# A transformer block on one core: attention and output projection in an order computed by a list scheduler at build time, and one merged score product for the first query tile

## The chip, the cores and the metric

The kernel runs on one core of a Trainium2 chip. A core has several engines that work side by side and wait for each other through semaphores: TensorE (PE in the profile, with its weight loads as PEld), VectorE (DVE), ScalarE (ACT), GpSimd (POOL) and SyncE (SP), which here issues the DMA transfers. The metric is the time of one execution on the device in microseconds; lower is better.

## The reference

One block of a transformer with 512 tokens (T) of width 1024, batch 1. Half of its 16 heads are "NSA" heads with three branches (compressed keys, selected keys, window), half attend within a sliding window of 128 with a learned sink. After attention come the output projection, a gated MLP with a short convolution, and a gated side input p.

```python
h = rmsnorm(x, attn_pre_g)
q_n, kc, vc, ksl, vsl, kwn, vwn, g_n, q_s, k_s, v_s = split(h @ w_in)
k_cmp, v_cmp = compress_kv(kc, ...), compress_kv(vc, ...)   # 31 blocks of 32 tokens
gates = sigmoid(g_n)
# NSA, per query: scores = q.k / 8 - slope * distance, causal
o_nsa = gates[0] * softmax(q k_cmp) v_cmp + gates[1] * softmax(q k_slc) v_slc \
      + gates[2] * softmax(q k_win) v_win
# sliding window: softmax over 128 keys and a sink in the denominator
o_swa = softmax([q_s k_s, sink]) v_s
x = x + rmsnorm(concat(o_nsa, o_swa) @ w_o, attn_post_g)
h = rmsnorm(x, mlp_pre_g)
a, u = split(h @ w_gate_up)
y = (gelu(causal_conv3(a)) * u) @ w_down
x = x + rmsnorm(y, mlp_post_g)
x = x + (p @ w_ple) * sigmoid(x @ w_ple_gate)
```

With 512 tokens there are 8 blocks to select from and 16 may be selected, so the selected branch sees every causal key, as the window of 512 does. 8 NSA heads share 2 key and value heads, and so do the 8 sliding-window heads. All is in float32.

## The kernel before, in words

**Numbers.** A float32 product is made of three products of rounded parts (`fp32r`): high with high, low with high, high with low (`mm3`, L147, L150, L151). So each weight is loaded raw (L140, tag `wr`, two buffers), its high part is cast on ScalarE (L128), and the low part is a difference on VectorE or GpSimd (L132). TensorE multiplies 128 rows by up to 512 columns into one PSUM bank.

**Stages.** Input and the natural-order values (to 33 us of the span), compression, key projections and the first three query projections (to 72), attention with the rest of the projections and the first half of the output projection (72 to 225), the second half of the output projection (225 to 249.5), the normalisation with the e = p·w_ple tiles (to 262), then the MLP and the gate.

**Attention.** 16 units are worked through: for NSA, and then for the sliding window, key group g = 0 and 1, and for each the query tiles qt = 3, 0, 2, 1 (128 queries, 4 heads each).

- *Scores* (`nsa_scores`, `swa_scores`). Two TensorE products per score piece, q with the high and the low part of the keys (L568, L569; `score`), into one of three PSUM banks (tag `s`). An NSA head's keys stand side by side in one tile `kn`: 32 compressed, 512 selected, 512 window keys. VectorE adds the distance bias and takes the minimum in one pass (L627, L595 for the window heads), ScalarE takes the exponential (L631), VectorE the reciprocal of the sum, GpSimd scales each row by it and by the gate (L537).
- *Values* (`pv`). Per 128 keys TensorE transposes the four heads' probabilities into one of two PSUM banks (L515, four transposes), ScalarE copies the high part out (L517), VectorE makes the low part (L519), and TensorE multiplies both with the values into the unit's one output bank (L548, two products per key block). `put_out` folds the output bank: a ScalarE copy (L526), two VectorE adds (L531), a ScalarE cast (L533) and a GpSimd difference (L534).

**What sets the order.** Each unit's scores and an earlier unit's value products are Python generators. `together` interleaves them by hand-written keys. After each step it calls `fill(ns)`, which adds credit at a hand-set rate (`RATES`, one for each group of units) and, while credit lasts, issues steps of 650 ns of the `fillers`: the projections of features 3, 8, 4, 5, 6, 7 (8 is the window keys; their results' low part on GpSimd in L389, then moved into place by DMAs on SP, L244), and after the first window unit `out_proj_first`. `pin` ties the first matmul of a filler step behind the attention step that was issued six steps earlier (`LAG`). Within those ties and the data's dependencies the framework's own scheduler, which simulates the engines, decides the order on each engine at build time. `keep_in_program_order` holds an instruction to the written order; in this part it is hardly used.

**Output projection.** For each of 8 columns c, `out_proj_first` sums k = 0 to 3 (the NSA half) and ScalarE copies the bank to `mo` (L798); `out_proj` then sums k = 4 to 7 and VectorE adds it (L827). Products are at L782 to L784. Each half column of the weight (`wo`, 256 KB) goes through `wr`, cast and difference (GpSimd in the first half, VectorE in the second). ScalarE squares the column (L236) and GpSimd sums the squares (L237; the last on VectorE) for the norm. In the second half, `ple_load` (p transposed and the two 512 KB weights `wple`, through `wr`) is called after c = 2, the reload of x (L241, four transfers of 512 KB) after c = 4.

Of the kernel before, what the change touches and what calls it, by code (L numbers as in the profile page):

```python
# [59 lines left out]
FILL_STEP = 650.0  # L60
WARM = 9
RATES = [0.36, 0.36, 0.9, 0.6]
LAG = 6
CYC = ["s", "o", "t", "t", "s", "mm", "s", "mm"]


class Block:
    def __init__(self, tc, io, ctx):
# [17 lines left out]
        self.fillers = []  # L86
        self.credit = 0.0
        self.rate = 1.0
        self.steps = [None]
        self.pinned = None  # L90
# [52 lines left out]
    def mm3(self, ps, wt, off, x, start, stop, keep=False):  # L143
# [3 lines left out]
        r = self.pin(mm(ps, hi, x[:, 0, :], start=start, stop=False))  # L147
# [4 lines left out]

    def pin(self, r):

        if self.pinned is not None:
            self.tc.add_manual_dep(r.ins, self.pinned.name, mybir.DependencyInfo(
                mybir.DependencyClass.NoSync, mybir.DependencyReason.DATA), reason="filler")
        return r
# [10 lines left out]


    def fill(self, ns):

        self.credit += ns * self.rate
        self.steps.append(self.steps[-1])
        while self.credit > 0 and self.fillers:
            self.credit -= FILL_STEP
            self.fill_step()

    def fill_step(self):
        phase, self.phase = self.phase, "fill"  # L180
        self.pinned = self.steps[max(0, len(self.steps) - 1 - LAG)]
        try:
            next(self.fillers[0])
        except StopIteration:
            self.fillers.pop(0)
        self.pinned = None
        self.phase = phase

    def drain(self, gen):
        while any(f is gen for f in self.fillers):  # L190
            self.fill_step()

    def att(self, r):
        self.steps[-1] = r.ins
        return r
# [180 lines left out]
    def proj(self, wt, f=None):  # L376
# [11 lines left out]
        eng = nc.gpsimd if self.phase == "fill" else nc.vector  # L388
        eng.tensor_sub(t[:, 1, :], v, t[:, 0, :].bitcast(F32))  # L389
# [91 lines left out]
    def compress_out(self, hk, hv):  # L481
# [13 lines left out]
        for g in range(2):  # L495
            z = [self.kn[g][i][:, 31:32] for i in range(2)]
            for a in z:
                nc.vector.memset(a.bitcast(F32), 0.0)
            hi, lo = self.kn[g][0][:, 0:31], self.kn[g][1][:, 0:31]
# [10 lines left out]
    def transpose_split(self, srcs, rows=P):  # L510

        nc = self.nc
        pt = self.ps("t")
        for r, src in enumerate(srcs):
            self.att(nc.tensor.transpose(pt[:rows, r * P : (r + 1) * P], src, self.ident))  # L515
# [23 lines left out]
    def pv(self, blocks, mix, qt):  # L539
# [22 lines left out]
        if last:  # L562
            product(n - 1, 1, False, True)
# [832 lines left out]
```

## Time and profile before

| | us |
|---|---|
| median of 3 runs (664.89 to 665.47) | 665.14 |
| the profiled execution's own time | 668.27 |
| its span | 666.5 |
| TensorE busy in the span | 652.6 (98%) |
| VectorE / ScalarE / GpSimd busy | 480.7 / 363.1 / 147.4 |
| attention, first score to the end of its half of the output projection | 72.3 to 225.2 |
| second half of the output projection | 225.2 to 249.5 |
| normalisation and e tiles | 249.5 to 262.0 |

A chain of waits is read from the top: a piece's start, its length, the engine or DMA that carried it, and its line. In a group, the numbers behind the first bar are the sum in us and the mean in ns, those behind the second the idle time ahead of the instructions and what ended it. In the timeline the bracket holds the idle time ahead of one instruction. All times of the profile are those of one execution; engines' "busy" counts a matmul from its issue on, with a modelled end.

### The profile page before, as it was taken

To read this page: it belongs to the slowest core of one execution; us is meant where nothing else is said; L and a number is where in the kernel's file an instruction comes from. 1 tells how busy PE (TensorE), PEld (TensorE's weight loads), DVE (VectorE), ACT (ScalarE), POOL (GpSimd) and SP (SyncE) were. 2 spreads that over 40 slices of the span, in tenths; PEclk is the share of its full clock that TensorE was granted. 3 is DMA by queue.
4 is the path that set the end of the run, shared out by engine and by line. 5 is a ranking of instruction groups with operands and counts; after the bars stand their busy time and mean duration, and the time that the engine had idled before them with its cause. 6 is when DMAs were issued, how large, how long until landed. Compare 5 with 4: busy or idle time off the path is not lost.

```text
span 666.5 us, 10339 instructions
## 1 busy us (share of the span) xinstructions
PE 652.6 (98%) x3741; PEld 565.5 (85%) x3741; DVE 480.7 (72%) x965; ACT 363.1 (54%) x684; POOL 147.4 (22%) x223
## 2 busy tenths in 40 slices
PE   8999999999999999999999999999999999999996
PEld 7988768777888777888887999999998888889985
DVE  6795777878757757858999999999958333224872
ACT  6554688878868737445555565565736323222351
POOL 1021568558556241003221000000000000001000
PEclk9999999999999999999999999999999999999999
DMA  8346721111121557412241332332244554332031
GB/s 299 115 139 213 199 64 47 34 48 49 48 73 56 179 206 269 173 57 95 95 160 63 127 109 83 128 117 76 95 144 156 153 209 143 88 111 71 1 127 63
DMA packets 27282, 78.01 MB, mean 117 GB/s; under 512 B 3424, under 2 KB 4704, under 8 KB 27232
## 3 DMA queue, kind: packets, MB, share of 16 engines
q1 hardware_dynamic: 27088, 77.28, 35.6%
q8 instruction: 29, 0.48, 0.3%
q14 instruction: 21, 0.17, 0.1%
q10 hardware_dynamic: 144, 0.08, 0.0%
HBM read 63.72 MB, written 6.29 MB: 105 GB/s over the span
## 4 chain that ended last, share of the span: by engine, by line
PE 79%; DVE 11%; ACT 4%; DMA 2%; issue 2%; POOL 1%; ACTq 0%; DVEq 0%
PE nsa_pso L548 3%; PE mlpdown_pss L147 3%; PE mlpdown_pss L150 3%; PE mlpdown_pss L151 3%; PE strassen_pss L1080 3%; PE strassen_pss L1084 2%; PE strassen_pss L1083 2%; PE nsa_pst L515 2%; PE mlpdown_psmm L147 2%; PE mlpdown_psmm L150 2%; PE mlpdown_psmm L151 2%; DMA outproj_wr<-in_wo_dram 2%; PE strassen_pst L1080 2%; PE strassen_pst L1083 2%; PE strassen_pst L1084 2%
## 5 line engine op out<-in xcount | busy, mean ns | idle before, releaser
L132 DVE TENSOR_TENSOR mlpdown_wh<-mlpdown_wr,mlpdown_wh 128x1024 fp32r<-128x1024 f32 (+1 forms) x28 | 32.3, 1158 | 48.6 <-ACT mlpdown_wh L128 47.6
L128 ACT ACTIVATE mlpdown_wh<-mlpdown_wr 128x1024 fp32r<-128x1024 f32 (+1 forms) x28 | 27.9, 998 | 63.5 <-PE mlpdown_pss L150 25.9
L237 POOL TENSOR_TENSOR mlpdown_s<-mlpdown_s,mlpdown_s 128x512 f32<-128x512 f32 x6 | 7.8, 1292 | 238.1 <-ACT mlpdown_s L236 238.1
L537 POOL TENSOR_SCALAR nsa_u<-nsa_u,nsa_nrc,gate 128x512 f32<-128x512 f32 (+3 forms) x64 | 38.2, 607 | 22.5 <-DVE nsa_nrc L662 16.7
L1080 PE MATMUL strassen_pss<-sums_u,strassen_u 128*128 128x256 f32 x144 | 40.6, 282 | 1.6 <-ACT strassen_s L1091 1.6
L1084 PE MATMUL strassen_pss<-sums_u,strassen_u 128*128 128x256 f32 x144 | 40.5, 281 | 0.0
L1083 PE MATMUL strassen_pss<-sums_u,strassen_u 128*128 128x256 f32 x144 | 40.5, 281 | 0.0
L631 ACT ACTIVATE nsa_u<-nsa_u,nsa_nnm 128x512 f32<-128x512 f32 (+3 forms) x64 | 35.4, 555 | 5.3 <-DVE nsa_nnm L627 5.0
L519 DVE TENSOR_TENSOR nsa_u<-nsa_pst,nsa_u 128x512 fp32r<-128x512 f32 (+1 forms) x43 | 29.0, 684 | 9.1 <-ACT nsa_u L517 8.8
L627 DVE CUSTOM_DVE_ANT_0 nsa_u<-nsa_pss,biastables_u 128x512 f32<-128x512 f32 (+3 forms) x64 | 29.9, 485 | 5.4 <-PE nsa_pss L569 5.0
L1042 DVE TENSOR_TENSOR strassen_u<-strassen_u,strassen_u 128x1024 fp32r<-128x1024 f32 x27 | 33.3, 1237 | 0.0
L517 ACT ACTIVATE nsa_u<-nsa_pst 128x512 fp32r<-128x512 f32 (+1 forms) x43 | 25.1, 591 | 13.2 <-PE nsa_pst L515 12.8
L147 PE MATMUL mlpdown_pss<-mlpup_u,mlpdown_wh 128*128 128x512 f32 (+1 forms) x88 | 32.0, 364 | 0.0
L150 PE MATMUL mlpdown_pss<-mlpup_u,mlpdown_wh 128*128 128x512 f32 (+1 forms) x88 | 32.0, 364 | 0.0
L151 PE MATMUL mlpdown_pss<-mlpup_u,mlpdown_wh 128*128 128x512 f32 (+1 forms) x88 | 32.0, 363 | 0.0
L132 POOL TENSOR_TENSOR fill_wh<-fill_wr,fill_wh 128x512 fp32r<-128x512 f32 (+1 forms) x14 | 24.7, 1762 | 33.0 <-ACT fill_wh L128 32.9
L1038 ACT ACTIVATE strassen_u<-strassen_u 128x1024 fp32r<-128x1024 f32 x27 | 28.4, 1051 | 1.2 <-DVE strassen_u L1054 1.1
L1080 PEld LDWEIGHTS strassen_pss<-sums_u,strassen_u 128*128 128x128 f32 x144 | 27.3, 190 | 1.9 <-ACT strassen_s L1091 1.8
L548 PE MATMUL nsa_pso<-nsa_u,vnatural_u 128*128 128x512 f32 x72 | 27.2, 441 | 0.9 <-ACT nsa_u L517 0.3
L1083 PEld LDWEIGHTS strassen_pss<-sums_u,strassen_u 128*128 128x128 f32 x144 | 27.2, 189 | 0.1
L1084 PEld LDWEIGHTS strassen_pss<-sums_u,strassen_u 128*128 128x128 f32 x144 | 27.2, 189 | 0.0
L1083 PE MATMUL strassen_pst<-sums_u,strassen_u 128*128 128x256 f32 x88 | 24.8, 282 | 0.0
(502 smaller groups left out, 2302.9 us busy)
## 6 DMA issues: line engine op xcount, KB each, us to landing
mlpdown_wr<-in_down_dram SPq DMA_DIRECT2D x16, 512.0 KB, 3.6
strassen_wr<-in_gu_dram SPq DMA_DIRECT2D x14, 512.0 KB, 4.6
strassen_u<-in_gu_dram SPq DMA_DIRECT2D x14, 512.0 KB, 3.9
mlpup_wr<-in_gu_dram SPq DMA_DIRECT2D x10, 512.0 KB, 3.3
fill_wr<-in_win_dram SPq DMA_DIRECT2D x6, 512.0 KB, 3.8
mlpdown_wr<-in_down_dram SPq DMA_DIRECT2D x8, 384.0 KB, 3.2
fill_u<-fill_u SPq DMA_DIRECT2D x20, 128.0 KB, 2.5
loadx_u<-in_xT_dram SPq DMA_DIRECT2D x8, 256.0 KB, 4.7
```

What stands on the lines that cost most here:

```text
L132: l = eng.tensor_sub(lw, raw, hi.bitcast(F32))
L147: r = self.pin(mm(ps, hi, x[:, 0, :], start=start, stop=False))
L150: mm(ps, lo, x[:, 0, :], start=False, stop=False)
L151: mm(ps, hi, x[:, 1, :], start=False, stop=stop)
L537: self.nc.gpsimd.tensor_scalar(ap, ap, col, gate, op0=ALU.mult, op1=ALU.mult)
L548: self.att(nc.tensor.matmul(po, v, rhs, start=start, stop=stop))
L627: nc.vector.tensor_tensor_reduce(dst, src, dist, op0=ALU.add, op1=ALU.min, scale=SLOPES[8 + 4 * g + r], scalar=3e38, accum_out=nm[:, r, b ...
L631: nc.scalar.activation(dst, dst, AF.Exp, bias=nm[:, r, b : b + 1], scale=-1.0, accum_out=sm[:, r, b : b + 1])
L1042: keep(sub(lo, src, hi.bitcast(F32)))
L1080: r = mm(ps, hi[:, o], x[:, 0, :], start=fresh and p == 0, stop=False, skip_group_check=not fresh)
L1083: mm(ps, lo[:, o], x[:, 0, :], start=False, stop=False, skip_group_check=not fresh)
L1084: mm(ps, hi[:, o], x[:, 1, :], start=False, stop=p == Q - 1, skip_group_check=not fresh)
```

## The change

**A planner.** A class `Plan` takes operations: a name, an engine, a duration in us (written as a constant or a line in the number of columns), a rank, a function that issues it, the operations it follows, and the buffers ("rooms") it takes and uses. `order` runs the engines forward: of all engines it takes the one whose next operation starts first, where an engine's next operation is that of lowest rank among those ready when it comes free (or that ready earliest); SP takes its list strictly by rank. A handoff between engines counts 0.17 us, from TensorE 0.33. A buffer counts as free when its users are done. `emit` issues the operations in the order of their planned start, and every one of them is held to that order by `keep_in_program_order` (of the three products of a projection step only the first).

**What is planned.** `plan_units` (all 16 units, in the same unit order as before; a unit's scores rank one unit ahead of its value products), `plan_projections` (features 3, 8, 4, 5, 6, 7; the weights of the first two are given ahead) and `plan_out` (both halves of the output projection). Scores, values and `put_out` are the same operations as before, each now an entry of the plan; projections and output projection rank behind all attention work on TensorE and so fill its gaps. Generators, `together`, `fill`, `pin`, `RATES` are gone.

**Merged scores.** For qt = 0 an NSA head needs 32 compressed, 128 selected and 128 window keys. `kn` is now laid out as two rows of 32 + 512 (selected, window), and one product reads columns 0 to 159 of both rows: 320 columns, one pair of products and one PSUM bank. Before it was two pairs of 256 columns and two banks.

**Output projection.** The first half of columns 0 to 4 (`EARLY`) is summed in two groups, k = 0, 1 and k = 2, 3, of which the second is added by VectorE: five more VectorE adds of 512 columns. `LATE_PS` names the PSUM banks of the second half. The sums of squares of columns 6 and 7 are on VectorE (before only 7). `wple` is loaded into slots of the pool `u` rather than `wr`; `ple_load` comes after the products of column 2, and the reload of x, by its place on SP, behind the last weight `wo`.

```diff
+    def order(self, free):
...
+            for eng, names in todo.items():
+                pick, f = None, free.get(eng, 0.0)
+                for name in names[:1] if eng == "SP" else names:
+                    r = ready(name)
+                    if r >= never:
+                        continue
+                    t = max(r, f)
+                    if pick is None or t < pick[0] - 1e-9:
+                        pick = (t, name)
+                    if t <= f + 1e-9:
+                        break
+                if pick and (best is None or pick[0] < best[0] - 1e-9):
+                    best = (*pick, eng)
...
-        eng = nc.gpsimd if self.phase == "fill" else nc.vector
-        eng.tensor_sub(t[:, 1, :], v, t[:, 0, :].bitcast(F32))
+        nc.vector.tensor_sub(t[:, 1, :], v, t[:, 0, :].bitcast(F32))
...
+    def plan_units(self, plan, qready):
...
+            S, V = i - 1.0, float(i)
...
+                segs = {0: [(0, 160, 2)], 3: [(0, 256, 1), (NCMP, T, 1), (NCMP + T, T, 1)]}.get(
+                    qt, [(0, NCMP + n, 1), (NCMP + T, n, 1)])
...
+                op(("t", i, j), "PE", 4 * 0.109, y, turn, dep, [("pt", ("pt", i, j))], use)
+                op(("h", i, j), "ACT", 0.475, y, high, [("t", i, j)], [("P", ("P", i, j))], [("pt", i, j)])
+                op(("l", i, j), "DVE", 0.607, y, low, [("h", i, j)], (), [("pt", i, j)])
...
+                    op(("v", i, j, 0), "PE", stream(T), y, lambda product=product: product(0), [("h", i, j), *more],
+                       [] if j else [("po", ("po", i))], [("P", i, j), ("po", i)])
...
+    def plan_out(self, plan, mixed):
...
+                groups = [range(4, 8)] if half else [range(0, 2), range(2, 4)] if c < EARLY else [range(0, 4)]
...
+        def total(c):
+            keep((nc.vector if c > 5 else nc.gpsimd).tensor_add(z["sq", 0], z["sq", 0], z["sq", c]))
...
+        for what, after in (("ple", ("op", 2, 7)), ("x1", ("op", 4, 4)), ("up", ("sa", 7)), ("up2", ("sa", 7))):
+            a(what, "X", 0.0, 0.0, lambda what=what: more(what), [after])
...
     def attention(self):
...
-        self.kn = [[self.u([P, NCMP + 2 * T], F32R, "kn") for i in range(2)] for g in range(2)]
+        self.kn = [[self.u([P, 2, NCMP + T], F32R, "kn") for i in range(2)] for g in range(2)]
...
+        plan = Plan({"p": 6, "P": 3, "ps": 3, "pt": 2, "po": 1, "mm": 2, "wr": 2, "wh": 6, "tt": 2, "s": 4, "as": 2, "un": UNITS, "u": 26})
...
+        order = [3, 8, 4, 5, 6, 7]
+        given = {f: self.proj_weight(f, "pool") for f in order[:2]}
+        ready = self.plan_projections(plan, order, {3: 1.0, 8: 4.5, 4: 4.6, 5: 4.7, 6: 8.0, 7: 8.2}, given)
+        mixed = self.plan_units(plan, ready)
+        z = self.plan_out(plan, mixed)
+        plan.emit(PE=0.0, SP=-8.0, DVE=2.0, ACT=1.0, POOL=-1.0)
...
-        return ph, [self.weight(io["wple"][j], tag=t) for j, t in enumerate(("pt", "u"))], e
+        return ph, [self.weight(self.raw(io["wple"][j], tag="u"), tag=t, early=True) for j, t in enumerate(("pt", "u"))], e
...
-        self.out_proj()
```

**The order on TensorE, first NSA unit's value products.** In the rows, `nsa_pst` is a bank of transposes, `nsa_pso` the output bank, `nsa_u` on the right the copied probabilities (here `nsa_u_978` is the copy of `nsa_pst_973`). Before:

```order
L548 MATMUL nsa_pso_938<-nsa_u_961,vnatural_u_334 128x512
L515 MATMUL nsa_pst_973<-ident,nsa_u_816 128x128
L515 MATMUL nsa_pst_973<-ident,nsa_u_850 128x128
L515 MATMUL nsa_pst_973<-ident,nsa_u_871 128x128
L515 MATMUL nsa_pst_973<-ident,nsa_u_892 128x128
L548 MATMUL nsa_pso_938<-nsa_u_944,vnatural_u_325 128x512
L515 MATMUL nsa_pst_986<-ident,nsa_u_816 128x128
L515 MATMUL nsa_pst_986<-ident,nsa_u_850 128x128
L515 MATMUL nsa_pst_986<-ident,nsa_u_871 128x128
L515 MATMUL nsa_pst_986<-ident,nsa_u_892 128x128
L548 MATMUL nsa_pso_938<-nsa_u_978,vnatural_u_343 128x512
L548 MATMUL nsa_pso_938<-nsa_u_961,vnatural_u_334 128x512
```

And now, for the same unit (`nsa_u_1034` is the copy of `nsa_pst_1022`, `nsa_u_1040` of `nsa_pst_1028`; `fill_psmm` is a projection):

```order
L763 MATMUL nsa_pst_1028<-ident,nsa_u_870 128x128
L763 MATMUL nsa_pst_1028<-ident,nsa_u_891 128x128
L234 MATMUL fill_psmm_980<-loadx_u_173,projq_wh_818 128x512
L237 MATMUL fill_psmm_980<-loadx_u_173,projq_wh_819 128x512
L238 MATMUL fill_psmm_980<-loadx_u_173,projq_wh_818 128x512
L781 MATMUL nsa_pso_1044<-nsa_u_1034,vnatural_u_325 128x512
L234 MATMUL fill_psmm_980<-loadx_u_183,projq_wh_818 128x512
L237 MATMUL fill_psmm_980<-loadx_u_183,projq_wh_819 128x512
L238 MATMUL fill_psmm_980<-loadx_u_183,projq_wh_818 128x512
L781 MATMUL nsa_pso_1044<-nsa_u_1034,vnatural_u_325 128x512
L781 MATMUL nsa_pso_1044<-nsa_u_1040,vnatural_u_334 128x512 x2
```

Between a bank's transposes and its products there now stand projection steps; before there stood one product and the next bank's transposes.

**The order on SP, output projection.** These are DMA issues (`wple` and `pT` belong to the e tiles, `wo` is the output projection's weight, `xT` the reload of x). Before:

```order
L241 DMA pletiles_u_2839<-in_pT_dram 128x1024
L140 DMA pletiles_wr_2851<-in_wple_dram 128x1024
L140 DMA pletiles_wr_2857<-in_wple_dram 128x1024
L140 DMA outproj_wr_2863<-in_wo_dram 128x512
L140 DMA outproj_wr_2886<-in_wo_dram 128x512
L241 DMA outproj_u_2909<-in_xT_dram 128x1024
L241 DMA outproj_u_2911<-in_xT_dram 128x1024
L241 DMA outproj_u_2913<-in_xT_dram 128x1024
L241 DMA outproj_u_2915<-in_xT_dram 128x1024
L140 DMA outproj_wr_2917<-in_wo_dram 128x512
L140 DMA outproj_wr_2940<-in_wo_dram 128x512
L140 DMA outproj_wr_2963<-in_wo_dram 128x512
```

Now:

```order
L921 DMA swa_wr_2737<-in_wo_dram 128x512
L227 DMA pletiles_u_2857<-in_wple_dram 128x1024
L227 DMA pletiles_u_2863<-in_wple_dram 128x1024
L921 DMA fill_wr_2764<-in_wo_dram 128x512
L921 DMA outproj_wr_2774<-in_wo_dram 128x512
L921 DMA outproj_wr_2801<-in_wo_dram 128x512
L921 DMA outproj_wr_2809<-in_wo_dram 128x512
L921 DMA outproj_wr_2835<-in_wo_dram 128x512
L294 DMA pletiles_u_2845<-in_pT_dram 128x1024
L921 DMA outproj_wr_2878<-in_wo_dram 128x512
L294 DMA outproj_u_2895<-in_xT_dram 128x1024
L294 DMA outproj_u_2897<-in_xT_dram 128x1024
```

The reload of x moved behind the last weight of the output projection, and the two `wple` transfers moved ahead of six of its weights.

**The order on GpSimd, entry of attention.** L132 (now L219 and L852) is the low part of a weight, L537 (now L563) scales probabilities. Before:

```order
L132 TENSOR_TENSOR fill_wh_829<-fill_wr_826,fill_wh_828 128x1024
L132 TENSOR_TENSOR fill_wh_835<-fill_wr_832,fill_wh_834 128x1024
L132 TENSOR_TENSOR fill_wh_1128<-fill_wr_1125,fill_wh_1127 128x1024
L537 TENSOR_SCALAR nsa_u_816<-nsa_u_816,nsa_nrc_814,gate 128x512 x2
L537 TENSOR_SCALAR nsa_u_850<-nsa_u_850,nsa_nrc_814,gate 128x512 x2
```

Now:

```order
L219 TENSOR_TENSOR projq_wh_813<-projq_wr_810,projq_wh_812 128x1024
L219 TENSOR_TENSOR projq_wh_819<-projq_wr_816,projq_wh_818 128x1024
L563 TENSOR_SCALAR nsa_u_826<-nsa_u_826,nsa_nrc_824,gate 128x512 x2
L852 TENSOR_TENSOR nsa_u_868<-nsa_wr_830,nsa_u_867 128x1024
L563 TENSOR_SCALAR nsa_u_849<-nsa_u_849,nsa_nrc_824,gate 128x512 x2
```

The third weight's low part moved behind the first two scalings.

More of the change, by code (lines that the diff above doesn't have):

```diff
@@ L146, in mm3 @@
         lo = wt[1][:, off : off + P]
-        r = self.pin(mm(ps, hi, x[:, 0, :], start=start, stop=False))
+        r = mm(ps, hi, x[:, 0, :], start=start, stop=False)
         if keep or self.ordered:
@@ L168, in gemm @@
             pass
[L171 to L195, printed above, removed]
     def rstd(self, acc, cname, copy=True):
@@ L507, in compress_out @@
         nc.scalar.activation(self.vc[32:63], self.vc[0:31].bitcast(F32), AF.Copy)
[L510 to L515, printed above, removed]
-        t = self.u([P, 2, T], F32R, "pt")
-        nc.scalar.activation(t[:rows, 0, :], pt[:rows], AF.Copy)
-        lo = t[:rows, 1, :] if rows == P else t[rows : 2 * rows, 0, :]
-        nc.vector.tensor_sub(lo, pt[:rows], t[:rows, 0, :].bitcast(F32))
-        return t
@@ L677, in mix_tiles @@
-    def mix_tiles(self):
-        return [self.u([P, 2, T], F32R) for _ in range(2)]
-    def together(self, *gens):
-        left = [(g, list(keys)) for g, keys in gens]
-        while left:
-            k = min(range(len(left)), key=lambda k: left[k][1][0] if left[k][1] else 0.0)
-            try:
-                ns = next(left[k][0])
-                left[k][1].pop(0)
-                self.fill(ns)
-            except StopIteration:
-                left.pop(k)
+    def scale_rows(self, ap, col, gate=1.0):
+        self.tc.keep_in_program_order(self.nc.gpsimd.tensor_scalar(ap, ap, col, gate, op0=ALU.mult, op1=ALU.mult))
@@ L713, in attention @@
         self.phase = "projk"
[L714 removed]
+        run(self.proj_k(self.proj_weight(10), lambda g, part: self.kn[g][part][:, 1, :T]))
         self.first_q(2)
         self.ks = [self.u([P, 2, T], F32R) for _ in range(2)]
[L718 to L734 removed]
@@ L771, in attention @@
-        while self.fillers:
-            self.fill_step()
-        for k in range(2, 4):
-            self.mix += [(mix[k][0][:, i, :], mix[k][1][:, i, :]) for i in range(2)]
-    def mixmm(self, ps, wt, ks, n0=0, end=True):
-        mm = self.nc.tensor.matmul
-        last = n0 + len(ks) - 1
-        for n, k in enumerate(ks, n0):
-            hi, lo = (w[:, n * P : (n + 1) * P] for w in wt)
-            xh, xl = self.mix[k]
-            self.pin(mm(ps, hi, xh, start=n == 0, stop=False))
-            mm(ps, hi, xl, start=False, stop=False)
-            mm(ps, lo, xh, start=False, stop=end and n == last)
-            yield
```

706 lines of the change are left out of this document (452 added, 254 removed).

## The prediction

> **What bounds the kernel now.** I read the page's busy table and chain first, then the view of stretches, then the chain of waits inside the part that the change touches.
>
> ```profile
> PE 652.6 (98%) x3741; PEld 565.5 (85%) x3741; DVE 480.7 (72%) x965; ACT 363.1 (54%) x684; POOL 147.4 (22%) x223
> PE 79%; DVE 11%; ACT 4%; DMA 2%; issue 2%; POOL 1%; ACTq 0%; DVEq 0%
> ```
>
> TensorE is busy for 98% of the span and carries 79% of the chain, so at first sight nothing is left to win by reordering. But the page warns that ends of matmuls are modelled: a matmul that waits for its weights counts as busy. What a stretch could have taken is its count of matmuls times the spacing at which they start when nothing waits. The stretches (length, then busy time and count of PE, PEld, DVE, ACT and POOL, clock, DMA share, GB/s):
>
> ```profile
> 72.30:225.20 152.90, 149.67 (x813) 119.88 (x812) 114.63 (x409) 122.63 (x325) 98.61 (x164) 1.00 0.26 73
> 225.20:249.50 24.30, 23.17 (x98) 17.59 (x98) 14.25 (x17) 10.11 (x17) 8.22 (x7) 1.00 0.55 184
> 249.50:262.00 12.50, 12.50 (x62) 10.27 (x60) 7.38 (x10) 8.48 (x13) 2.97 (x3) 1.00 0.69 220
> 530.00:600.00 70.00, 70.00 (x312) 57.81 (x311) 21.98 (x21) 18.95 (x21) 5.17 (x4) 1.00 0.43 139
> 380.00:480.00 100.00, 100.00 (x845) 100.00 (x844) 98.12 (x152) 59.85 (x93) 0.00 (x0) 1.00 0.31 104
> ```
>
> The first three rows are attention, the second half of the output projection, and the normalisation behind it. The last two are undisturbed: in the down projection 312 matmuls of 512 columns fill 70 us, about 0.227 us each once the two or so counted at both edges are taken off; in the Strassen part 845 of 256 columns fill 100 us, 0.119 each. Transposes and the odd product with the compressed values are read from these rows of the chain and of the timeline:
>
> ```profile
> 193.58 0.87 PE swa_pst L515 x8
> ```
> ```profile
> 99.22 0.50 PE L548 MATMUL nsa_pso<-nsa_u,vc 64*128 64x512 f32 x1
> 99.66 0.50 PE L548 MATMUL nsa_pso<-nsa_u,vnatural_u 128*128 128x512 f32 x1
> ```
>
> Eight transposes in 0.87 us are 0.109 each; the product with 64 rows holds up its successor by 0.2 us beyond 0.227. The counts between 72.3 and 249.5 us, line by line in the view of stretches (transposes L515, value products L548, first of two score products L568, first of three in a projection L147 and in the output projection L782; the second number in brackets counts weight loads):
>
> ```profile
> 72.30:249.50 177.20, 37.40 (x248) 28.90 (x248) 1.00 0.30 88
> 72.30:249.50 177.20, 41.88 (x116) 19.64 (x116) 1.00 0.30 88
> 72.30:249.50 177.20, 33.68 (x104) 19.59 (x104) 1.00 0.30 88
> 72.30:249.50 177.20, 19.40 (x48) 9.07 (x49) 1.00 0.30 88
> 72.30:249.50 177.20, 25.40 (x64) 11.95 (x64) 1.00 0.30 88
> ```
>
> 512 wide: 116 + 3 × 48 + 3 × 64, and by the loops 32 scores of the last query tile, 484 × 0.227 = 109.9 us. Transposes: 248 × 0.109 = 27.0. By the loops 128 scores are 256 wide, 15.2, and 16 each are 416, 384 and 288 wide, 7.9 on the line through 0.119 at 256 and 0.227 at 512. With 8 × 0.2 for the compressed values that is 161.6 us of 177.2: **15.6 us in which TensorE had work and waited**. The output projection's half is 96 × 0.227 = 21.8 of 24.3 us, so 2.5 of it lie there and 13.1 in attention. The chain inside one unit of attention shows what such time looks like:
>
> ```profile
> 90.99 0.73 PE nsa_pso L548 x2
> 91.72 0.65 PE nsa_pst L515 x4
> 92.38 0.47 PE nsa_pso L548 x2
> 92.84 0.54 PE nsa_pst L515 x4
> 93.38 0.48 PE nsa_pso L548 x2
> ```
>
> Two products and four transposes should take 2 × 0.227 + 4 × 0.109 = 0.89 us. From 90.99 to 93.38 two such rounds take 2.39 instead of 1.78: each is a little late for ScalarE's copy or VectorE's difference. In the first two stretches the other engines stay below TensorE (ScalarE 122.6 + 10.1 of 177.2 us, VectorE 128.9, GpSimd 106.8), so an order that hands TensorE something else to do can take most of the 15.6 us away.
>
> **The change, part by part.** *Merged scores.* For the first query tile a head's two branches cost two pairs of 256 columns, 4 × 0.119 = 0.476 us; one pair of 320 columns costs 2 × 0.146 on the same line. Eight heads (two groups of four) save 8 × 0.184 = **1.5 us**. If the two-piece pattern of columns streamed as slowly as 512 columns, 0.2 us would be left.
>
> *Attention's order (13.1 us of waiting).* No instruction is taken away but those scores; what changes is how much TensorE work stands between a producer and its use. That can be counted in the two orders with the spacings above. What is needed, by the timeline and a group:
>
> ```profile
> 116.24 0.60 PE L515 MATMUL nsa_pst<-ident,nsa_u 128*128 128x128 f32 x4
> ...
> 116.93 1.22 ACT L517 ACTIVATE nsa_u<-nsa_pst 128x512 fp32r<-128x512 f32 x2 [2.20 <-PE nsa_pst L515]
> ...
> 117.22 0.69 DVE L627 CUSTOM_DVE_ANT_0 nsa_u<-nsa_pss,biastables_u 128x512 f32<-128x512 f32 x1 [0.32 <-PE nsa_pst L515]
> ...
> 117.58 0.73 PE L548 MATMUL nsa_pso<-nsa_u,vnatural_u 128*128 128x512 f32 x2
> ```
> ```profile
> L531 DVE TENSOR_TENSOR nsa_s<-nsa_pso,nsa_s 64x256 f32<-64x256 f32 x14 | 5.8, 413 | 1.0 <-ACT nsa_s L526 0.9
> ```
>
> The four transposes have had their slots at 116.24 + 0.44 = 116.68; an idle ScalarE starts at 116.93 and the first product at 117.58, 0.90 us after the slots. With a VectorE difference of 0.68 behind it a second product needs 1.56. The reuse of one of three score banks needs a VectorE pass of 0.69 and the 0.25 ahead of it, about 1.0; that of the only output bank 0.25, a ScalarE copy of 0.61 and two adds of 0.41, with a handoff about 1.8. Less work than that stands there in the order before at 14 of 62 first products, 8 of 85 reuses of a score bank, 7 of 60 of a transpose bank: 5.8 us short in sum, where 13.1 are lost, 2.25 times as much, since these engines also queue and TensorE refills its weights after each wait. In the new order it is 1 first product, 1 second product (1.12 instead of 1.56), 1 score bank, no transpose bank, and two output banks (0.87 and 1.35 instead of 1.8): 1.9 us short. At the same ratio 4.3 are lost: **8.8 us saved**. Bounds: all 13.1 if every handoff is covered; 4.5 if each shortage left costs twice as much again (2 × 4.3 = 8.6 still lost). I take 8.8 since the count is of the same kind on both sides.
>
> *Entry.* In front of the first softmax VectorE is held:
>
> ```profile
> 73.66 2.41 POOL L132 TENSOR_TENSOR fill_wh<-fill_wr,fill_wh 128x1024 fp32r<-128x1024 f32 x1 [3.04 <-ACT fill_wh L128]
> 74.24 2.37 DVE L389 TENSOR_TENSOR projq_u<-projq_s,projq_u 128x512 fp32r<-128x512 f32 x1
> ```
> ```profile
> L519 DVE TENSOR_TENSOR nsa_u<-nsa_pst,nsa_u 128x512 fp32r<-128x512 f32 (+1 forms) x43 | 29.0, 684 | 9.1 <-ACT nsa_u L517 8.8
> ```
>
> A difference that takes 0.68 us from a bank takes 2.37 between two tiles while GpSimd works. In the new order GpSimd makes that third weight only after the first two scalings, so this one shrinks to 0.7; its gain is inside the 13.1.
>
> *Output projection (2.5 us).* Before, its weights queue on SP behind the reload of x:
>
> ```profile
> 228.76 2.22 SPq L241 DMA_DIRECT2D outproj_u<-in_xT_dram  x4
> 231.37 10.05 SPq L140 DMA_DIRECT2D outproj_wr<-in_wo_dram  x3
> ...
> 231.37 8.26 DMA outproj_wr<-in_wo_dram
> ```
> ```profile
> pletiles_wr<-in_wple_dram SPq DMA_DIRECT2D x2, 512.0 KB, 3.6
> L862 DVE SCALAR_TENSOR_TENSOR fill_u<-fill_u,cols,r_pst x8: 739/742/748, 259.6 to 274.4; 128x512 f32<-128x512 f32 x8
> ```
>
> A load that lands in 2.66 us two rows earlier in this chain takes 8.26 here. Now the four loads of x follow the last weight, which is issued some 12 us before the product's end; x is first used at 259.6, 10 us after that end, so the move costs nothing as long as they land within 20 us. But two loads of 512 KB for the e product (wple) now stand ahead of six of the eight second-half weights, they wait for a TensorE release, and both their ScalarE casts and VectorE differences stand ahead of the third group's. Five VectorE adds of 0.68 us are new (the first half of five columns is now summed in two pieces); VectorE has room. I put the third and fifth group 0.6 us late each, 1.2 in all: **1.3 us saved**, bounds 2.5 saved and 1.0 lost.
>
> ```profile
> 227.24 2.66 DMA outproj_wr<-in_wo_dram
> 241.00 1.30 POOL L237 TENSOR_TENSOR outproj_s<-outproj_s,outproj_s 128x512 f32<-128x512 f32 x1 [3.80 <-ACT outproj_s L236]
> 241.41 1.43 DVE L132 TENSOR_TENSOR outproj_wh<-outproj_wr,outproj_wh 128x512 fp32r<-128x512 f32 x1 [0.35 <-ACT outproj_wh L128]
> ```
>
> Against this part speaks the last pair: a weight difference on VectorE met a GpSimd sum of squares and took 1.43 us instead of 0.7. [...] What it would do here: five GpSimd sums remain beside the eight differences, five meetings of 0.7 us; a group of weights is due every 12 × 0.227 = 2.7 us, so nothing shows while each has that much lead, and 3.5 us if none has: then 2.2 lost here instead of 1.3 saved.
>
> *Behind it* the same eight e tiles fill the wait for the norm (12.5 us, of which their 48 products need 10.9): 0, bounds 1 saved and 0.5 lost. The rest of the program stands in the same order on TensorE and only starts earlier.
>
> Sum: 8.8 + 1.3 + 1.5 = 11.6 us. The profiled execution took 668.27 us for a span of 666.5; it would be 656.7. Off the median of 665.14 it is **653.5 us**.
>
> **Rivals.** *The waits move rather than go* (0.22): ScalarE has 122.6 us in attention's 152.9; in 141 it would be 87% full, and an order planned to the tenth leaves its queue no slack. For it: ScalarE is named in the waits above. Against: the distances grew almost everywhere. Then attention gives 4.5 and the 2.2 of those meetings is lost behind it: 3.8 with the merge, 661.3; with half of that effect, 657.5.
> *Nearly all waits go* (0.13): 12.5 + 2 + 1.5 = 16, 649. For it: Strassen's part, also ordered by hand, runs at its spacing.
> *The output projection starves* (0.10): the e weights on SP wait for the release of a slot by TensorE, and six weight loads queue behind them. If that release is the last product of the first half, two loads of 3.6 us (median in the page's list of issues), one of 2.66, a cast of 0.61 and a difference of 1.43 follow, 11.9 us, of which TensorE has two groups, 5.4, to do: 6.5 lost, 660.3 with the gain before it. If x is also late by the 8.26 that a load behind it took, 14.8 are lost and 10.3 won: 669.6, slower. It decides from a release later than 10 us before the projection's end of first half; a slot of a finished query tile would be far earlier, so I give 0.06 to slower and 0.04 to no change.
> *It does not do what it says*: only the first of three products is held in order; but the built order keeps the triples together, so I give this no chance of its own.
>
> **Numbers.** Forecast (8 to 14 us saved) 0.55, its own range 651 to 657; smaller gain 0.22, larger 0.13, starved 0.10. The range takes both neighbours in: from 16.5 saved to 4 saved, **648.5 to 661**. A change within 0.2% (1.3 us) can't be told from none: faster 0.90, same 0.04, slower 0.06.
>
> **What would show it.** The stretch from the first score to the first e tile should be about 165.5 us, from 177.2, with 16 matmuls fewer (32 of 256 columns gone, 16 of 320 new). In a unit's products, rounds of 0.89 us with a triple of 0.68 between, not 1.0 to 1.4. The wait of VectorE at the entry about 0.7. If the output projection's eight groups take over 24.3 us, the loads were late; if ScalarE ends most waits of TensorE in attention, the first rival holds; an earlier start that is lost again before Strassen's part would mean a second path that I have not seen.

## The result and the profile after

The changed kernel takes 661.61 us (median of 10 runs, 659.92 to 665.51) against 665.58 us for the kernel before (10 runs, 664.87 to 668.13): a ratio of 0.994, 95% interval 0.9918 to 0.9962, so 2.5 to 5.5 us faster. In a later set of runs it was 0.9932 (0.9911 to 0.9952). The forecast was 653.5, with a range from 648.5 to 661: the sign is right, the gain is a third of what was forecast, and the time lies just outside the range.

The page of the changed kernel, busy engines and chain:

```profile
PE 644.6 (98%) x3725; PEld 564.6 (86%) x3725; DVE 478.2 (72%) x971; ACT 361.1 (55%) x684; POOL 145.5 (22%) x222
PE 88%; DVE 4%; DMA 3%; ACT 3%; issue 1%; SPq 0%; ACTq 0%; DVEq 0%
```

The chain runs through TensorE for 88% of the span instead of 79%: VectorE's pieces, which made 11% of it, are down to 4%. The stretches tell how much of that is time. From the first score to the end of the output projection, the e tiles behind it, and the MLP's first part up to Strassen's part, whose tiles are named `strassen` (columns as before: length, busy time and count of PE, PEld, DVE, ACT, POOL, clock, DMA share, GB/s):

```profile
70.60:238.70 168.10, 165.16 (x894) 136.99 (x892) 125.65 (x431) 130.51 (x341) 106.81 (x171) 1.00 0.30 90
238.70:254.10 15.40, 14.12 (x61) 11.35 (x60) 7.24 (x10) 8.22 (x12) 1.04 (x1) 0.89 0.56 192
254.10:344.30 90.20, 88.98 (x397) 73.20 (x396) 76.66 (x109) 46.56 (x66) 15.00 (x8) 1.00 0.37 132
```

| stretch | before | after | gain |
|---|---|---|---|
| before the first score | 72.3 | 70.6 | 1.7 |
| attention and output projection | 177.2 | 168.1 | 9.1 |
| e tiles, until the MLP's first product | 12.5 | 15.4 | -2.9 |
| MLP until Strassen's part | 89.0 | 90.2 | -1.2 |
| the rest (to 666.5 and 659.7) | 315.5 | 315.4 | 0.1 |

So the planned part gains 9.1 of the 11.6 us, and **4.1 us of it are given back right behind it**. The 1.7 us at the entry are not the change's: over the 14 profiled executions of all kernels the first score comes either at 70.4 to 70.6 us (six of them) or at 72.0 to 72.6 (eight), the same program on either side, and the profile of before was of the later sort. Without them the profiles differ by 5.1 us, which agrees with the timed interval.

In attention the rounds look as forecast where nothing is late. The chain inside a unit:

```profile
118.53 0.47 PE nsa_pso L781 x2
119.00 0.44 PE nsa_pst L763 x4
119.44 0.23 PE nsa_pso L781
119.67 0.44 PE nsa_pst L763 x4
```

Four transposes take 0.44 us and a product 0.23, their spacing without waits; in the chain before, four transposes took 0.54 to 0.65 and two products 0.47 to 0.73. The merged scores run as costed, 0.145 us apart (129.22, 129.37, 129.51 in the timeline):

```profile
129.22 0.31 PE L567 MATMUL nsa_pss<-compress_u,projq_u 128*128 128x320 f32 x1
129.37 0.31 PE L568 MATMUL nsa_pss<-compress_u,projq_u 128*128 128x320 f32 x1
129.51 0.30 PE L567 MATMUL nsa_pss<-compress_u,projq_u 128*128 128x320 f32 x1
```

With 1.5 us less to do, TensorE needs 160.1 us of the 168.1: 8.0 us of waiting where there were 15.6. None of it is in the second half of the output projection, which takes 21.8 us (216.9 to 238.7) for 96 products that need 21.8. So attention's waits fell from 13.1 to 8.0 us.

What is lost behind the projection begins on SP. Before, the four MLP weights (`gu`) were issued behind the projection's last weights, from 6.6 us before its end (249.5) on, and took 3.2 us from issue to landing (median):

```profile
242.87 9.31 SPq L140 DMA_DIRECT2D outproj_wr<-in_gu_dram  x4
outproj_wr<-in_gu_dram SPq DMA_DIRECT2D x4, 512.0 KB, 3.2
```

Now they follow right behind the four loads of x, from 7.4 us before the end (238.7) on:

```profile
228.52 2.64 SPq L294 DMA_DIRECT2D outproj_u<-in_xT_dram  x4
231.26 14.16 SPq L227 DMA_DIRECT2D outproj_wr<-in_gu_dram  x4
```

The chain shows what that does:

```profile
231.26 9.67 DMA outproj_wr<-in_gu_dram
...
243.25 0.68 DVE fill_u L949
...
245.09 5.54 DMA outproj_wr<-in_gu_dram
250.63 0.02 issue
250.65 1.07 ACT outproj_wh L215
251.72 0.02 issue
251.74 0.05 DVE outproj_wh L219
...
252.88 0.75 DVE swa_u L1070
```

and in VectorE's timeline:

```profile
242.11 1.22 DVE L219 TENSOR_TENSOR outproj_wh<-outproj_wr,outproj_wh 128x1024 fp32r<-128x1024 f32 x1 [3.35 <-ACT outproj_wh L215]
243.25 0.68 DVE L949 TENSOR_TENSOR fill_u<-fill_u,outproj_pss 128x512 f32<-128x512 f32 x1
```

The projection's last product ends near 239. The add of its last column (L949) starts at 243.25, because the low part of the first MLP weight (L219) stands ahead of it in VectorE's order, and that weight, loaded behind the four loads of x, took 9.67 us to land. The first step of the normalisation (L1070, 252.88) in turn stands behind the low part of the fourth weight, which landed at 250.63. TensorE has the e tiles to do meanwhile, but the square sum waits for the last column, so it stops for 1.4 us near 244.4. And then this happens:

```profile
247.68 0.63 PE L234 MATMUL r_pss<-pletiles_u,pletiles_wh 128*128 128x512 f32 x1
248.11 0.63 PE L237 MATMUL r_pss<-pletiles_u,pletiles_wh 128*128 128x512 f32 x1
```
```profile
247.20:250.60 3.40, 3.40 (x9) 2.63 (x9) 1.30 (x2) 0.53 (x1) 1.04 (x1) 0.50 0.87 311
```

Products start 0.43 us apart instead of 0.227: the granted clock is 0.50 for 3.4 us, which alone costs 1.7 us of TensorE time. This is no steady part of the loss: of the ten executions only this one and one other have a mean clock as low as 0.995, the rest 0.998 to 1.0.

### The profile page after: what moved, and what is told of

Its sections match the earlier page's. It is cut to its first block, busy times and chain, and to the rows that moved or that the text cites. A ratio compares the mean times of both kernels' runs of the same rounds, so it can differ in the third digit from the quotient of the medians.

```text
span 659.7 us, 10315 instructions
## 1 busy us (share of the span) xinstructions
PE 644.6 (98%) x3725; PEld 564.6 (86%) x3725; DVE 478.2 (72%) x971; ACT 361.1 (55%) x684; POOL 145.5 (22%) x222
## 4 chain that ended last, share of the span: by engine, by line
PE 88%; DVE 4%; DMA 3%; ACT 3%; issue 1%; SPq 0%; ACTq 0%; DVEq 0%
PE nsa_pst L763 3%; PE nsa_pso L781 3%; PE mlpdown_pss L234 3%; PE mlpdown_pss L238 3%; PE mlpdown_pss L237 3%; PE strassen_pss L1288 3%; PE strassen_pss L1292 3%; PE strassen_pss L1291 3%; DMA outproj_wr<-in_gu_dram 2%; PE mlpdown_psmm L234 2%; PE mlpdown_psmm L237 2%; PE mlpdown_psmm L238 2%; PE mlpup_pss L238 2%; PE fill_psmm L237 2%; PE fill_psmm L234 2%; PE fill_psmm L238 2%
## 5 line engine op out<-in xcount | busy, mean ns | idle before, releaser
L219 DVE TENSOR_TENSOR mlpdown_wh<-mlpdown_wr,mlpdown_wh 128x1024 fp32r<-128x1024 f32 (+1 forms) x28 | 32.4, 1161 | 48.3 <-ACT mlpdown_wh L215 47.3
L772 DVE TENSOR_TENSOR nsa_u<-nsa_pst,nsa_u 128x512 fp32r<-128x512 f32 (+1 forms) x48 | 31.9, 685 | 16.5 <-ACT nsa_u L767 16.1
L563 POOL TENSOR_SCALAR nsa_u<-nsa_u,nsa_nrc,gate 128x512 f32<-128x512 f32 (+3 forms) x64 | 38.6, 620 | 20.3 <-DVE nsa_nrc L672 8.0
L767 ACT ACTIVATE nsa_u<-nsa_pst 128x512 fp32r<-128x512 f32 (+1 forms) x48 | 27.4, 591 | 13.9 <-PE nsa_pst L763 13.4
L1291 PE MATMUL strassen_pst<-sums_u,strassen_u 128*128 128x256 f32 x88 | 24.8, 281 | 0.0
L1288 PE MATMUL strassen_pst<-sums_u,strassen_u 128*128 128x256 f32 x88 | 24.8, 281 | 0.0
```

The costliest lines, as they stand in the source:

```text
L219: l = eng.tensor_sub(lw, raw, hi.bitcast(F32))
L563: self.tc.keep_in_program_order(self.nc.gpsimd.tensor_scalar(ap, ap, col, gate, op0=ALU.mult, op1=ALU.mult))
L772: keep(nc.vector.tensor_sub(d, u["pt", j][:rows], t[:rows, 0, :].bitcast(F32)))
L1288: r = mm(ps, hi[:, o], x[:, 0, :], start=fresh and p == 0, stop=False, skip_group_check=not fresh)
L1291: mm(ps, lo[:, o], x[:, 0, :], start=False, stop=False, skip_group_check=not fresh)
```

## The experiments

The runs below were made on three chips, and each ratio is to the kernel before on the same chip (medians 667.35, 667.4 and 665.84 us). The changed kernel ran again only on the first, so later runs are set against it by way of the ratios. The yardstick first: the changed kernel unaltered.

> The changed kernel unaltered, as the yardstick beside the others on the same chip. Its two profiled losses, 3.8 us of waiting in the e tiles (238.7 to 254.1) and some 5 us of TensorE waiting between 164 and 192, should be there again if they belong to the program; if they belonged to that one execution, they move or vanish. Expected ratio to the kernel before: 0.994.

Ratio 0.9932 (0.9911 to 0.9952), 662.2 us. The loss is there again, with a granted clock of 1.00 in all three stretches: e tiles 14.8 us, MLP's first part 90.4, attention and projection 168.9 (a score of the first unit waited 1.3 us for the transfer of its keys, where it had waited 0.5). Of the 4.1 us, 3.7 are lost here too, so the loss belongs to the program.

**The reload of x, moved away from the MLP's weights.**

```diff
-        for what, after in (("ple", ("op", 2, 7)), ("x1", ("op", 4, 4)), ...
+        for what, after in (("ple", ("op", 2, 7)), ("x1", ("t", 14, 1)), ...
```

> The changed kernel with the four loads of x moved from behind the last output-projection weight to the end of the window heads, where the DMA share was 0.02. Theory 1 (the loads of x share the DMA engines with the first two MLP weights, whose load took 9.67 us): those two weights land within about 4 us, the e tiles' stretch falls from 15.4 to about 12 us and the start of the MLP no longer waits: 4 us faster than the changed kernel. Theory 2 (what counts is only that VectorE's add of the last column stands behind the first MLP weight's difference): that row is still behind it, and the gain is what the earlier landing gives there, also up to 4. If neither holds (the norm's own chain sets the MLP's start): under 1 us.

Ratio 0.9894 (0.9877 to 0.991), 2.5 us below the changed kernel by the medians. The stretches:

```profile
70.60:239.40 168.80, 165.47 (x893) 136.73 (x892) 125.91 (x431) 131.03 (x341) 105.89 (x171) 1.00 0.32 92
239.40:252.90 13.50, 12.72 (x61) 10.13 (x60) 8.31 (x13) 8.27 (x13) 2.21 (x2) 1.00 0.68 225
252.90:342.00 89.10, 88.91 (x397) 73.19 (x397) 75.64 (x107) 46.18 (x65) 15.01 (x8) 1.00 0.37 128
```

The first MLP weight lands in 3.3 us (issued at 232.08, landed at 235.37). The e tiles lose 1.9 us less and the MLP's start 1.1 less: 3.0 of the 4.1 us, by these two profiles (2.5 by the medians), are due to where x is reloaded. The rest stays because the second weight was issued only at 237.21 and landed after the projection's end, and its difference still stood ahead of the last column's add.

**VectorE's order alone.**

```diff
-                self.upw = [self.weight(io["gu"][i]) for i in range(2)]
+                self.upw = [self.weight(io["gu"][i], keep=True) for i in range(2)]
```

> The changed kernel, with the casts and differences of the first two MLP weights held behind the last column's add and sum; no load is moved. Theory 2 (VectorE's queue): the last add moves from 243.25 to about 239.5, the norm is ready some 3.5 us earlier, and the time falls by 2 to 4 us. Theory 1 (the loads are late whatever VectorE does): the MLP still waits for the third and fourth weight, which landed at 246.7 and 250.6, and the gain is 0 to 1 us.

Ratio 0.9918 (0.9897 to 0.9939), 1.2 us below the changed kernel by the medians, which is not clear of the noise. The last add moved to 239.93, as wanted, 1.1 us behind the projection's end. But the e tiles still take 14.7 us. The chain now goes through ScalarE:

```profile
244.91 5.21 DMA outproj_wr<-in_gu_dram
250.13 0.02 issue
250.15 1.06 ACT outproj_wh L215
251.21 2.44 ACT pletiles_u L1132 x5
```

The copies that empty the e tiles' banks (L1132) stand behind the cast of the fourth weight, and wait for its load. So the order on VectorE was one place where the late loads showed; with it mended they showed at the next. With the run before, which moved only loads, this makes the late loads the cause.

**The first half of every column in one group.**

```diff
-EARLY = 5
+EARLY = 0
```

> The changed kernel with the first half of every column summed in one group (EARLY = 0): five VectorE adds fewer, and no output-projection product before both NSA halves are there. Theory 3 (ScalarE is full in the window heads, whatever TensorE is given): the attention part changes by under 1 us. Rival (the early products cost a weight cast on ScalarE at the worst place): up to 2 us faster, as the planner's own costs put it. Rival (the early groups are needed as filler): 1 to 3 us slower.

> The same program as in the earlier run with the first half of each column in one group, as the yardstick for the next two on the same chip. Expected ratio to the kernel before: 0.986, and 0.7 us of waiting in the e tiles; if the first run was a lucky chip, 0.990.

Ratios 0.986 (0.9837 to 0.9882) and 0.9857 (0.9838 to 0.9877): 5 us below the changed kernel in both sets. The second run's stretches:

```profile
70.40:236.90 166.50, 164.55 (x894) 136.83 (x894) 121.98 (x425) 130.49 (x341) 106.78 (x171) 1.00 0.32 94
236.90:249.10 12.20, 12.20 (x61) 10.26 (x60) 8.92 (x12) 8.46 (x14) 1.04 (x1) 1.00 0.66 218
249.10:338.30 89.20, 89.01 (x398) 73.23 (x397) 75.72 (x107) 46.19 (x65) 15.00 (x8) 1.00 0.36 130
```

Only 1.6 us of it is in attention and projection; 3.2 are in the e tiles and 1.0 in the MLP's start, so the whole loss is gone, with x reloaded at the same place in SP's order. The reason shows in VectorE's rows for the fourth of the second half's eight weights, of the changed kernel (the projection's second half begins at 216.9) and of this one (215.1):

```profile
222.54 0.69 DVE L929 TENSOR_TENSOR outproj_u<-outproj_wr,outproj_u 128x512 fp32r<-128x512 f32 x1
```
```profile
216.69 0.69 DVE L929 TENSOR_TENSOR outproj_u<-fill_wr,outproj_u 128x512 fp32r<-128x512 f32 x1 [2.03 <-ACT outproj_u L925]
```

Its difference starts 1.6 us after the half's start instead of 5.6. All loads on SP follow in one order, so p, x and the MLP's weights move forward too: the first of these lands 0.7 us before the projection's end instead of 2.2 after it. That the two-group columns hold weight buffers until their second group, and so delay the next loads, is argued from the code; no run took the five adds away without the grouping.

**Is ScalarE the limit in the window heads?**

```diff
-    ... self.exp(u["pk", 0][:, r, : n + 1], u["nm"][:, r : r + 1], u["sm"][:, r : r + 1])
+    ... keep(nc.scalar.activation(p, p, AF.Exp, bias=u["nm"][:, r : r + 1], scale=-1.0))
-    nc.vector.reciprocal(u["rc"], u["sm"])
+    nc.vector.reciprocal(u["rc"], u["nm"])
```

> The changed kernel in the same planned order, but the window heads' exponentials no longer sum their rows (VectorE inverts the minimum instead of the sum): the softmax of the window heads is not normalised. ScalarE loses 32 reads of 0.19 us, some 6 us, between 155 and 205 us, where it was busy for 38 of 41 us. Theory 3 (ScalarE is full there and TensorE waits for it): TensorE's waits between 160 and 200 fall from about 5 us to under 2, and the stretch from the first score to the end of the projection falls from 168 to 164 or 165. Rival (the order itself, or VectorE, makes those waits): the stretch stays at 167 to 168.

Ratio 0.9916 (0.9897 to 0.9935), about 1 us below the changed kernel, which is not clear of the noise. Between 160 and 200 us, of the changed kernel and of this one:

```profile
160.00:200.00 40.00, 37.57 (x224) 30.61 (x223) 33.98 (x111) 36.61 (x108) 26.52 (x53) 1.00 0.16 49
```
```profile
72.60:240.00 167.40, 164.93 (x893) 137.15 (x892) 124.67 (x430) 128.32 (x309) 105.81 (x171) 1.00 0.31 90
160.00:200.00 40.00, 38.05 (x229) 31.28 (x228) 34.68 (x116) 35.73 (x83) 27.36 (x55) 1.00 0.16 47
```

The edit freed less of ScalarE than was expected. With 25 reads fewer it is still busy for 35.7 of these 40 us instead of 36.6 (this execution runs 2 us later, so the work in them is not quite the same), and over the whole stretch for 128.3 us instead of 130.5. The reason is that a read's row overlaps the rows of the exponentials: one after the other they start 0.49 us apart (180.26, 180.76, 181.25 in the changed kernel), and each read starts 0.40 us behind its exponential (180.66). By these rows a read holds the next exponential up by 0.09 us, and 32 reads are worth an estimated 2.9 us and not 6. The stretch to the projection's end is 167.4 us (168.1 and 168.9 in the two executions of the changed kernel), not 164 or 165: taking 2.2 us off ScalarE gave 0.7 to 1.5. What a ScalarE with more room would give, no run shows. Who ends TensorE's waits in attention can be read from the changed kernel's four longest groups (sum, times, longest, in us):

```profile
PE nsa_pso L781 <- DVE nsa_s L809: 1.1, 1, 1.1
PE swa_pso L781 <- ACT swa_u L767: 0.6, 1, 0.6
PE nsa_pss L568 <- DMA compress_u<-projk_u: 0.5, 1, 0.5
PE swa_pst L763 <- DVE swa_u L772: 0.3, 1, 0.3
```

Without the reads the wait of 0.6 us for ScalarE is gone, and the longest is the same. It is the first product of a unit, for the only output bank, one of the two places that the prediction had counted as short (0.87 us of work, the eight transposes that stand there, where 1.8 are needed). The adds that free this bank start at 169.36, 0.5 us after ScalarE's copy has ended: VectorE has three bias passes of the window heads before them.

**Longer handoffs in the plan.**

```diff
-    LAG = 0.17
-    LAGPE = 0.33
+    LAG = 0.25
+    LAGPE = 0.45
```

> The changed kernel planned with longer handoffs (0.25 us between engines for 0.17, 0.45 from TensorE for 0.33), nothing else. If the many small waits left in attention (63 of 30 to 100 ns, 5.3 us in sum) come from handoffs planned too short: 2 to 4 us faster in attention. If the queues' fullness sets them: no change or 1 us slower.

Ratio 0.9902 (0.9884 to 0.992). The stretches (attention, second half of the projection, e tiles):

```profile
72.10:220.00 147.90, 145.28 (x798) 118.47 (x797) 113.44 (x414) 119.06 (x323) 98.90 (x163) 1.00 0.26 71
220.00:242.40 22.40, 22.04 (x97) 17.91 (x96) 12.17 (x17) 10.58 (x17) 8.08 (x8) 1.00 0.67 231
242.40:255.00 12.60, 12.60 (x62) 10.13 (x60) 8.45 (x11) 9.18 (x14) 1.04 (x1) 1.00 0.61 205
```

Attention is not faster, 147.9 us where the changed kernel has 146.3 (70.6 to 216.9), so nothing here shows that the small waits come from handoffs planned too short. Yet the kernel is no slower than the changed one, by the medians 1.6 us faster (660.61 against 662.2, with intervals that overlap): the first MLP weight lands 0.3 us after the projection's end instead of 2.2, and the e tiles take 12.6 us instead of 14.8 or 15.4. The MLP starts at 255.0, in the changed kernel's execution with the same late entry at 255.7. A slower attention that costs nothing fits with loads, not attention, setting when the MLP began.

**The merge undone, and the merge alone in the kernel before.**

```diff
-                segs = {0: [(0, 160, 2)], 3: ...
+                segs = {0: [(0, 256, 1), (NCMP + T, 256, 1)], 3: ...
-                where = {0: [(0, 0, NCMP), (0, NCMP, n), (0, 160, n)], 3: ...
+                where = {0: [(0, 0, NCMP), (0, NCMP, n), (1, 0, n)], 3: ...
```

> The changed kernel with the first query tile's two branches in two products of 256 columns each, as before; the planner orders the rest anew. By the spacings (0.119 at 256 columns, 0.145 measured at 320) the merge saves 8 x 0.186 = 1.5 us of TensorE: 1 to 2 us slower than the changed kernel if that is all; 0 if the attention part is limited by other engines, since those have the same work; over 3 if the third bank per head matters.

Ratio 0.9968 (0.9952 to 0.9983) beside the changed kernel's 0.9932: about 2.4 us slower.

```diff
+            if qt == 0:
+                ps = self.ps("s")
+                self.score(ps, ps[:, :320].rearrange("p (a n) -> p a n", a=2), lhs, *(t[:, :, :160] for t in k2))
```

> The kernel before, with only the merged score product of the first query tile. The sum of the prediction says 1.5 us less TensorE work: 663.5 to 664.5 where the kernel before has 665 to 667. If undoing the merge in the changed kernel (3.2 us slower than the changed kernel) showed the merge's worth and not an unlucky new order of the planner: 3 us faster. If other engines bound the first query tile: no change.

Ratio 1.0047 (1.0027 to 1.0068): **slower**, by 3.1 us. The first stretches of both, with the merge undone and with the merge alone:

```profile
70.60:220.40 149.80, 145.41 (x814) 119.98 (x813) 113.12 (x412) 119.31 (x323) 99.50 (x164) 1.00 0.25 70
```
```profile
72.10:228.70 156.60, 150.80 (x797) 119.06 (x796) 114.34 (x409) 122.44 (x325) 98.60 (x164) 0.99 0.25 71
```

Without the merge attention takes 149.8 us instead of 146.3, with the merge alone 156.6 instead of the 152.9 of before. Both moved by over 3 us, against 1.5 of TensorE work, and in one case the wrong way. Each edit makes the scheduler order everything anew, and the new order's waits outweigh the 1.5 us. With the merge undone the second half of the projection also takes longer, 23.6 us for 21.8, but the e tiles 12.5 for 15.4: of 5.3 us lost, 2.9 come back behind the projection. In the kernel before with the merge, TensorE stops for 1.6 us near 86 and then runs at a granted clock of 0.50 for 3.3 us, which is 1.7 of its 3.7 us:

```profile
88.70:92.00 3.30, 3.30 (x12) 2.60 (x11) 1.52 (x3) 1.06 (x1) 2.52 (x7) 0.50 0.00 0
```

So the merge's columns are worth 1.5 us as counted, but no run isolates its worth in time.

**Edits together.** Three of them (one group, x moved, VectorE's order):

> The changed kernel with three edits together: the first half of each column in one group, x reloaded at the end of the window heads, the first two MLP weights' differences behind the last column's add. Alone they measured 4.8, 2.5 and 1.2 us less than the changed kernel. If all three work on one loss (the wait behind the projection, 5 us in all): 656 to 657, hardly better than the best alone. If they add up: 653 to 654.

Ratio 0.9896 (0.9878 to 0.9914): worse than the one-group kernel alone. Attention and projection take the same 166.5 us, but the e tiles 14.0: as in the run on VectorE's order, the copies of L1132 stand behind the late weights' casts. Then the two without that edit:

> The first half of each column in one group, and x reloaded at the end of the window heads; VectorE's order is left to the scheduler. If the loads of the MLP weights are what is late behind the projection: 1 to 2 us below the one-group kernel alone. If holding the weights' differences back (the third edit of the three taken together) was what made those three slower than the one edit alone, this is at least 2 us below them. If the two edits work on one loss: same as the one-group kernel.

Ratio 0.9856 (0.9835 to 0.9876), the same as the one-group kernel (0.9857 on the same chip). The edits repair one loss, and once it is gone there is nothing left for the second.

**The load of p, moved as well.**

```diff
+        ..., ("x1", ("t", 14, 1)), ("pT", ("t", 15, 1)), ...
```

> As the run before, and the load of p with its casts and differences also moved to the end of the window heads. In the changed kernel its two VectorE differences waited for that load at 231 us and stood ahead of three column adds and a weight difference that frees the buffer of the next load. If that queue holds back the MLP weights: the first two land at least 2 us before the projection's end and the time is 1 to 2 us below the run before. If not: no change.

Ratio 0.9986 (0.9973 to 0.9999): nearly all is lost again. The chain:

```profile
205.81 8.16 DMA pletiles_u<-in_pT_dram
213.96 0.02 issue
213.99 0.64 ACT pletiles_u L1123
```

The load of p, issued behind the four loads of x (2 MB), takes 8.16 us, and the scheduler put its casts ahead of a window unit's copies on ScalarE and its differences ahead of that unit's adds on VectorE; TensorE waited 7.0 us before that unit's products. The e tiles take 12.2 us in this kernel, but attention pays for it. It is the loss behind the projection once more, in another place: a load and the instruction that consumes it, put early in an engine's order.

The best version is the one with `EARLY = 0` (655.71 us where the kernel before has 665.84 on the same chip), faster than both kernels (ratio 0.9857, 0.9838 to 0.9877, where the changed kernel has 0.9932, 0.9911 to 0.9952).

## Why the prediction was wrong, by its steps

- **What bounds the kernel: right.** 15.6 us of waiting between the first score and the projection's end, to be had by order alone; 7.6 of them went, and 9.2 with one group per column (166.5 us, 160.1 needed).
- **Merged scores, 1.5 us: right in columns** (0.145 us a product against 0.146), unproven in time.
- **Attention's order, 8.8 us: too much.** 13.1 fell to 8.0, 5.1 saved, just inside the bounds (4.5 to 13.1). The step that failed is the ratio of 2.25 between work short and time lost, taken over from the old order: 1.9 us short lost 8.0, not 4.3. Counting the work in front of each product sees only TensorE's side. The output bank's place was found (1.1 us waited). There VectorE's own queue added 0.5 us. Of the rest, 2.2 us less work on ScalarE gave 0.7 to 1.5 us and longer planned handoffs none; the remainder is many small waits whose cause stays open.
- **Entry: right.** VectorE's difference took 0.69 us, from 2.37:

```profile
72.51 0.69 DVE L441 TENSOR_TENSOR projq_u<-projq_s,projq_u 128x512 fp32r<-128x512 f32 x1 [0.74 <-ACT projq_u L440]
```

- **Output projection, 1.3 us: the sign right, the size too small.** All 2.5 were saved. The e weights ahead of the projection's weights delayed nothing on TensorE. Meetings of VectorE and GpSimd were there, differences of 1.21 instead of 0.69 us (at 226.87 and 234.06, each while a GpSimd sum ran), and cost nothing, since each weight had a lead.
- **"Behind it: 0, bounds 1 saved and 0.5 lost": this is the step that failed most.** 4.1 us were lost (3.7 in the second execution). The prediction moved the four loads of x behind the last weight and asked only when x itself is needed (it was in time: landed at 239.6, first used at 253.7). It did not ask what is queued behind those loads on SP: the four MLP weights, the first of which then took 9.67 us, and whose casts and differences stand ahead of the norm in both engines' orders. Reading on in SP's order, behind the place to which the loads moved, would have shown it. With 5.1 for 8.8, 2.5 for 1.3 and -4.1 for 0, the sum 11.6 becomes 5.0.
- **Rivals.** "The waits move rather than go" (0.22, 661.3) came, and its time was right, but by another mechanism: the waits moved behind the projection, to late loads. In attention ScalarE ended 0.6 of the 2.5 us of waits listed above, VectorE 1.4, and the meetings of VectorE and GpSimd cost nothing. The starved projection did not come. (Its sum is off by 1 us: 10.3 won and 6.5 lost give 661.3, not 660.3.) The text named "an earlier start that is lost again before Strassen's part" as the sign of a path not seen; that is what the stretches show. The range stopped at 661.0 with this rival's time at its edge: the unknown cost behind the projection had bounds that were much too narrow.

## What to carry to other kernels

When a transfer is moved, read the queue behind its new place as well as its own deadline: the transfers that follow it, and every engine on which their consumers stand ahead of something urgent. When a stage is made shorter, look for what was paced by its length; here the next stage's weights were, and a kernel with a slower attention was no slower in the end. And where a scheduler reorders all after each edit, one edit's worth is known only to a few us: judge by the stretch in which it acts, not by the end time.

## What the runs showed of the hardware

The granted clock of TensorE fell after waits. Their length is given here as the rows and stretches have it, from the modelled end of the last matmul on (1.28 us for the wait of 1.4 near 244.4, 1.48 for the one of 1.6 near 86). In the changed kernel the clock was 0.50 from 247.2 to 250.6; the wait of 1.28 us had ended at 245.81. In the kernel before with the merge it was 0.50 from 88.7 to 92.0; the wait of 1.48 us had ended at 87.97. In the run on VectorE's order the products from 255.10 to 256.80 start 0.43 us apart, and the 90.5 us from 253.5 on have a mean clock of 0.98; in the 14.7 us of e tiles ahead of them TensorE was idle for 2.2 us in all.

As much idle time also came without a fall: 1.8 us in the e tiles of the changed kernel's second execution (busy 12.99 of 14.80), 1.5 us there with three edits together (12.52 of 14.00), 1.6 us in the second half of the projection with the merge undone (22.01 of 23.60). The clock of each of these stretches and of the one behind it is 1.00. In the run with p moved, the products behind the wait of 7.0 us start 0.43 us apart (217.50, 217.93, 218.36), and the mean clock of the 154.4 us up to 226.7 is 0.97. What sets the fall off, these runs do not show.
